# A batched row gather: four direct batches instead of five, index groups of 2, 2 and then 3, a ring of ten buffers, the seventh batch half-loaded, and first products between the index groups

## The chip, the cores and the metric

One core of one Trainium2 chip. The metric is the device time of one execution in microseconds (us); the profiler's span of the same execution is about 1.8 us shorter. Each result is compared with runs of the kernel before on the same chip and in the same rounds. "Fast" and "slow" are states of a run; for one core a run is called slow when it is over 1.5% above the fastest run of its kernel.

## The reference

```python
# x: (32, 512, 1024) float32, indices: (32, 128) int32
for b in range(32):
    result[b] = x[b, indices[b]]
```

Of each batch, 128 rows of 4 KB are picked, with repeats. Some 114 of the 128 are distinct. The kernel gathers each distinct row once into a slot and makes the repeats with a 0/1 matrix on TensorE.

## The kernel before

The first batches (`HEAD`) are gathered "directly", with their repeats, straight from the index list. For the others ("ring batches") three index steps come first, for a group of batches at a time: find the first occurrence of each index (`step0`: search on VectorE), number them (`step1`: rank), and put row numbers into slots (`step2`: slots, and the matrix `s` that spreads the slots over the output rows). A gather then fills a ring buffer, two products of 128x512 spread it, ScalarE copies the result from PSUM, and a store writes it. Batch `HALF` is special: its first 256 rows are loaded whole, early, without indices; its products have two more parts ("early products"), and its gather is half as long.

```python
HEAD, RING, GROUP, AHEAD, FAR = 5, 8, 3, 4, 1024
HALF = HEAD
# ...
pbc  = ctx.enter_context(tc.tile_pool(name="pbc",  bufs=2, space=PS))
psm  = ctx.enter_context(tc.tile_pool(name="psm",  bufs=1, space=PS))
pout = ctx.enter_context(tc.tile_pool(name="pout", bufs=4, space=PS))
# ...
for b in range(HEAD):
    gather(blocks[b], first[...] if b == 0 else idxT[:, b:b + 1], b)
    store(b)
# ...
def fetch(b):                      # gather into the ring, by the slots' row numbers
    if HEAD <= b < B:
        gather(held[(b - HEAD) % RING][:], at[:, b:b + 1], b, bounds_check=S - 1, oob_is_err=False)
# ...
def half_rows(h, last):            # the half batch: early part, or the last part and the copy
    w = slice(h * 512, (h + 1) * 512)
    if not last:
        spread[HALF, h] = pout.tile([N, 512], F32, name="ps")
    ps = spread[HALF, h]
    if last:
        pe(mm, ps[:], lhsT=spread[HALF], rhs=held[(HALF - HEAD) % RING][:, w], start=False, stop=True)
    else:
        for k in range(2):
            pe(mm, ps[:], lhsT=spread[HALF, "early"][k], rhs=early[k][:, w], start=k == 0, stop=False)
    if last:
        nc.scalar.copy(out=blocks[HALF][:, w], in_=ps[:])
# ...
step0(0)
step0(1)
for g in range(AHEAD):             # four groups, 12 batches, ahead of the first ring product
    step1(g)
    if 0 < g < AHEAD - 1:
        step0(g + 1)
    step2(g)
    for b in of_group(g):
        if b < HEAD + RING:
            fetch(b)
    if g == 0:
        half_spread()
    elif g < 3:
        half_rows(g - 1, False)    # early products between the index steps
for b in range(HEAD, B):
    spread_rows(b)
    fetch(b + RING)
    g, step = divmod(b - HEAD, GROUP)
    if g + AHEAD < GROUPS:
        (step0, step1, step2)[step](g + AHEAD)
```

The kernel holds each engine to the order of instructions written here.

## Time and profile before

| | kernel before |
|---|---|
| time | 87.41 us median of 3 (87.31 to 88.5) |
| span of the profiled run | 85.6 us |
| bytes moved by DMA | 32.91 MB |
| DMA rate from 13 us on | 416 to 419 GB/s |
| TensorE busy, 20 to 32 us | 11.98 of 12.00 us |

In the table by stretch, the last figure of a line is the DMA rate in GB/s, the one before it the busy share of the 16 DMA engines. A line of a timeline has the start and the length in us, the engine, the operation, and in brackets how long the engine was idle before it and what ended that. What the rest of the page says is read in the prediction below. Three more lines of the GpSimd timeline before give the gathers, the twelfth to the fourteenth:

```profile
18.97 1.00 POOL L121 DMA_INDIRECT u<-in_x_dram,at  x1 [1.50 <-issue]
20.27 1.00 POOL L121 DMA_INDIRECT u<-in_x_dram,at  x1 [0.30 <-issue]
22.34 1.00 POOL L121 DMA_INDIRECT u<-in_x_dram,at  x1 [1.07 <-PE bc L24]
```

### The profile page before, as it was taken

How to read it: one execution, taken by the hardware profiler on the slowest of the kernel's cores; microseconds unless marked ns; L12 is line 12 of the kernel's file. 1: busy time of each engine (PE TensorE's matmuls, PEld its weight loads, DVE VectorE, ACT ScalarE, POOL GpSimd, SP SyncE). 2: the span in 40 equal slices, each digit the busy share in tenths (PEclk: the TensorE clock that was granted, in tenths of full speed). 3: DMA queues.
4: the chain of work that ended last, by engine and by line, in shares of the span. 5: the costliest groups of instructions: out<-in, count | busy, mean ns of one | idle time of the engine just before them, and what ended most of it. 6: DMA issues, size and time to landing. Idle time of an engine off the chain costs nothing.

```text
span 85.6 us, 827 instructions
## 1 busy us (share of the span) xinstructions
PE 61.3 (72%) x189; PEld 25.3 (29%) x189; DVE 31.6 (37%) x160; ACT 40.5 (47%) x63; POOL 33.3 (39%) x43
## 2 busy tenths in 40 slices
PE   0320379576999999999878987878789888889300
PEld 0300242323434444444333433322223333323000
DVE  4498793786563864844641453000000000000000
ACT  0899930000665665555554354455544554446400
POOL 6587578727444455554332444443320000000000
PEclk9999999999999999999999999999999999999996
DMA  0799999999999999999999999999999999999980
GB/s 1 274 375 344 302 342 415 415 417 417 419 419 419 417 421 419 415 419 417 419 419 419 417 419 413 421 413 423 417 417 419 419 419 419 423 415 417 423 337 15
DMA packets 9636, 32.91 MB, mean 384 GB/s; under 512 B 1584, under 2 KB 1616, under 8 KB 9632
## 3 DMA queue, kind: packets, MB, share of 16 engines
q1 hardware_dynamic: 4736, 16.81, 48.2%
q0 software_dynamic: 4608, 15.01, 44.7%
q10 hardware_dynamic: 288, 1.05, 3.3%
q8 instruction: 1, 0.02, 0.1%
q14 instruction: 3, 0.02, 0.1%
HBM read 17.86 MB, written 16.78 MB: 404 GB/s over the span
## 4 chain that ended last, share of the span: by engine, by line
DMA 40%; PE 21%; issue 14%; DVE 14%; POOL 3%; ACT 1%; SPq 0%; POOLq 0%; DVEq 0%
DMA u<-in_x_dram,at 37%; PE ps L24 20%; DVE junk L24 3%; POOL u L121 3%; DVE pack L24 3%; DMA vals<-in_indices_dram 2%; DVE past L24 2%; DVE nth L24 2%; DVE s L24 1%; PE pos L24 1%; DVE slot L24 1%; ACT block L250 1%; DVE lead L24 1%; DVE same L24 1%; SPq L68 0%
## 5 line engine op out<-in xcount | busy, mean ns | idle before, releaser
L24 PE MATMUL ps<-u,s 128*128 128x512 f32 x108 | 52.4, 611 | 6.8 <-DMA u<-in_x_dram,at 6.2
L121 POOL DMA_INDIRECT u<-in_x_dram,at x27 | 26.9, 997 | 26.7 <-PE ps L24 5.8
L250 ACT COPY block<-ps 128x512 f32<-128x512 f32 x36 | 21.1, 585 | 18.7 <-PE ps L24 17.6
L24 PEld LDWEIGHTS ps<-u,s 128*128 128x128 f32 x108 | 18.3, 189 | 29.1 <-ACT block L250 14.8
L250 ACT COPY pair<-ps 128x512 f32<-128x512 f32 x16 | 9.4, 585 | 8.7 <-PE ps L24 7.1
L24 DVE SCALAR_TENSOR_TENSOR junk<-bc,idxF,below 128x128 f16<-128x128 f32 x27 | 8.0, 347 | 7.1 <-PE bc L24 7.1
L24 ACT COPY u<-zero 128x1024 f32<-128x1024 f32 x8 | 7.7, 1040 | 0.0
L24 PE MATMUL pos<-near,pack 128*128 128x1 f16 x27 | 2.0, 167 | 5.6 <-DVE pack L24 5.6
L240 ACT COPY block<-ps 128x512 f32<-128x512 f32 x2 | 1.2, 585 | 10.1 <-PE ps L24 10.1
L24 PE MATMUL ps<-early,same 128*128 128x512 f32 x8 | 5.7, 854 | 0.0
L24 DVE TENSOR_TENSOR pack<-turn,slot 128x384 f16<-128x384 f16 (+2 forms) x10 | 5.1, 518 | 0.3
L24 DVE TENSOR_TENSOR s<-bc,at 128x384 f32<-128x384 f32 x9 | 5.0, 558 | 0.3
L24 PEld LDWEIGHTS <-pack 128*128 128x128 f16 x27 | 1.7, 99 | 9.5 <-DVE pack L24 7.4
L24 DVE TENSOR_TENSOR past<-past,lead 128x1 f16<-128x1 f16 x25 | 4.1, 163 | 0.9
L24 PE MATMUL bc<-vf,ident 128*128 128x128 f16 x27 | 3.4, 256 | 1.3 <-DVE same L24 1.3
L121 POOL DMA_INDIRECT block<-in_x_dram,idxT x4 | 3.8, 947 | 1.3 <-issue 0.9
L24 PEld LDWEIGHTS <-ident 128*128 128x128 f16 x27 | 2.4, 111 | 4.2 <-issue 4.2
L24 DVE TENSOR_SCALAR at<-pos 128x3 int32<-128x3 f32 x9 | 1.4, 160 | 5.1 <-PE pos L24 4.8
L24 DVE CAST nth<-rk 128x3 int32<-128x3 f32 x9 | 1.4, 160 | 3.7 <-PE rk L24 3.3
L21 PE MATMUL pos<-ident,vf 128*128 128x32 f16 x1 | 0.2, 210 | 3.6 <-DVE vf L24 3.6
L24 ACT ACT_TABLE_LOAD x1 | 1.3, 1283 | 2.5 <-DVE vf L24 2.5
L24 PEld LDWEIGHTS ps<-early,same 128*128 128x128 f32 x8 | 1.9, 257 | 1.5 <-issue 1.5
(32 smaller groups left out, 18.4 us busy)
## 6 DMA issues: line engine op xcount, KB each, us to landing
out_dram<-block SPq DMA_DIRECT2D x24, 512.0 KB, 8.0
out_dram<-pair SPq DMA_DIRECT2D x4, 1024.0 KB, 11.1
early<-in_x_dram ACTq DMA_DIRECT2D x2, 512.0 KB, 3.8
u<-in_x_dram,at POOLq DMA_INDIRECT x27, 15.2
block<-in_x_dram,idxT POOLq DMA_INDIRECT x4, 6.4
vals<-in_indices_dram SPq DMA_DIRECT2D x1, 32.0 KB, 2.0
first<-in_indices_dram SPq DMA_DIRECT2D x1, 1.0 KB, 1.8
block<-in_x_dram,first POOLq DMA_INDIRECT x1, 5.2
```

What stands on the lines that cost most here:

```text
L21: self.last = do(*args, **kw)
L24: self.last = do(*args, **kw)
L121: nc.gpsimd.indirect_dma_start(out=dst, out_offset=None, in_=xf[:], in_offset=bass.IndirectOffsetOnAxis(ap=at, axis=0), element_offset=b * ...
L240: nc.scalar.copy(out=blocks[HALF][:, w], in_=ps[:])
L250: nc.scalar.copy(out=blocks[b][:, w], in_=ps[:])
```

## The change

The intent: the first ring gather should not wait for an index group of three, so the first groups have two batches and their `past` counting is off their path; one batch less is gathered with repeats; more gathers can be issued ahead of the products (ring of ten); and the first products are placed where their data lands, between the index groups. With that the half batch becomes the third ring batch, and its early products are no longer done apart. The core of the diff (index arithmetic of the ranks, the order tables and the split of `step2` into `fill_slots` and `match` are cut):

```diff
-    HEAD, RING, GROUP, AHEAD, FAR = 5, 8, 3, 4, 1024
-    HALF = HEAD
+    HEAD, RING, GROUP, FAR = 4, 10, 3, 1024
+    HALF = HEAD + 2
...
+    groups = [range(HEAD, HEAD + 2), range(HEAD + 2, HEAD + 4),
+              *(range(b, b + GROUP) for b in range(HEAD + 4, B, GROUP))]
...
-    def half_rows(h, last):
-        ...
+    def spread_rows(b, halves=range(2)):
+        for h in halves:
             w = slice(h * 512, (h + 1) * 512)
             ps = pout.tile([N, 512], F32, name="ps")
+            parts = [(spread[b], held[(b - HEAD) % RING])]
+            if b == HALF:
+                parts = [*zip(spread[b, "early"], early), *parts]
+            for i, (s, u) in enumerate(parts):
+                pe(mm, ps[:], lhsT=s, rhs=u[:, w], start=i == 0, stop=i == len(parts) - 1)
             nc.scalar.copy(out=blocks[b][:, w], in_=ps[:])
...
     step0(0)
-    step0(1)
-    for g in range(AHEAD):
-        ...
+    for g in range(2):
+        step1(g)
+        spread_indices(g + 1)
+        fill_slots(g)
+        fetch_group(g)
+        find_leads(g + 1)
+        match(g)
+    step1(2)
+    fill_slots(2)
+    fetch_group(2)
+    half_spread()
+    spread_indices(3)
+    match(2)
+    find_leads(3)
+    spread_rows(HEAD)
+    step1(3)
+    spread_rows(HEAD + 1)
+    spread_indices(4)
+    fill_slots(3)
+    fetch_group(3)
+    find_leads(4)
+    match(3)
+    step1(4)
+    spread_rows(HALF, [0])
+    spread_indices(5)
+    fill_slots(4)
+    for b in groups[4][:2]:
+        fetch(b)
+    find_leads(5)
+    match(4)
+    spread_rows(HALF, [1])
+    ...
```

More of the change, by code (lines that the diff above doesn't have):

```diff
@@ L48 @@
     N = indices.shape[1]
-    HEAD, RING, GROUP, AHEAD, FAR = 5, 8, 3, 4, 1024
-    HALF = HEAD
+    HEAD, RING, GROUP, FAR = 4, 10, 3, 1024
+    HALF = HEAD + 2
     PAIRED = range(12, 20)
-    GROUPS = (B - HEAD) // GROUP
-    assert 2 * N <= S <= FAR and (B - HEAD) % GROUP == 0
+    APART = B - 2
+    groups = [range(HEAD, HEAD + 2), range(HEAD + 2, HEAD + 4),
+              *(range(b, b + GROUP) for b in range(HEAD + 4, B, GROUP))]
+    assert HALF in groups[1] and 2 * N <= S <= FAR and groups[-1][-1] == B - 1
     const = ctx.enter_context(tc.tile_pool(name="const", bufs=1))
@@ L76 @@
     nc.gpsimd.iota(rank[:, 0], pattern=[[8, 2], [64, 2], [1, 8], [16, 4]], base=0, channel_multiplier=0)
-    for p0, p1, at0 in ((0, 36, 0), (36, 48, 112), (48, 104, 36), (104, 108, 124), (108, N, 92)):
+    for p0, p1, at0 in ((0, 38, 0), (52, 71, 44), (77, 104, 63), (105, N, 90), (71, 77, 121), (104, 105, 127)):
         nc.gpsimd.iota(rank[:, 1, p0:p1], pattern=[[1, p1 - p0]], base=at0, channel_multiplier=0)
+    twos = rank[:, 1, 38:54].rearrange("p (k a l) -> p k a l", a=2, l=2)
+    nc.gpsimd.iota(twos[:, :3, 1], pattern=[[2, 3], [1, 2]], base=38, channel_multiplier=0)
+    nc.gpsimd.iota(twos[:, :, 0], pattern=[[2, 4], [1, 2]], base=113, channel_multiplier=0)
     less = const.tile([N, 1], F32, name="less")
@@ L151, with wide, dealt_on, spread_indices @@
     nth, at = table("nth", I32), table("at", I32)
-    past = const.tile([N, B + 1], F16, name="past")
-    for b in (HEAD, B - 1):
-        dve(v.memset, past[:, b:b + 1], 0.0)
+    past = const.tile([N, len(groups)], F16, name="past")
     bcs, packs, spread = {}, {}, {}
-    def of_group(g):
-        return range(HEAD + g * GROUP, HEAD + (g + 1) * GROUP)
     def cols(t, g):
-        return t[:, HEAD + g * GROUP:HEAD + (g + 1) * GROUP]
-    def wide(t):
-        return t.rearrange("p (g o) -> p g o", o=1).to_broadcast([N, GROUP, N])
-    def step0(g):
+        return t[:, groups[g][0]:groups[g][-1] + 1]
+    def wide(t, n):
+        return t.rearrange("p (g o) -> p g o", o=1).to_broadcast([N, n, N])
+    def dealt_on(g):
+        return sum(b < APART for b in groups[g])
+    def spread_indices(g):
         bcs[g] = bc = pbc.tile([N, 4, N], F32, name="bc")
-        for k, b in enumerate(of_group(g)):
+        for k, b in enumerate(groups[g]):
             pe(mm, bc[:, k], lhsT=ident[:, b:b + 1].to_broadcast([N, N]), rhs=vf[:], start=True, stop=True)
-        for k, b in enumerate(of_group(g)):
+        if g == 0:
+            pe(mm, bc[:, GROUP], lhsT=ident[:, 0:1].to_broadcast([N, N]), rhs=turn[:, 0], start=True, stop=True)
+    def find_leads(g):
+        bc = bcs[g]
+        for k, b in enumerate(groups[g]):
             junk = junkp.tile([N, N], F16, name="junk")
@@ L174, in step0 @@
                 op0=ALU.is_equal, op1=ALU.mult, accum_out=cnt[:, b:b + 1])
-        if HALF in of_group(g):
+        if HALF in groups[g]:
             c = slice(HALF, HALF + 1)
@@ L179, in step0 @@
         dve(v.tensor_scalar, out=cols(lead, g), in0=cols(cnt, g), scalar1=0.0, scalar2=None, op0=ALU.is_equal)
-        for b in of_group(g):
-            if b < B - 2:
-                dve(v.tensor_tensor, out=past[:, b + 1:b + 2], in0=past[:, b:b + 1], in1=lead[:, b:b + 1], op=ALU.add)
+    def step0(g):
+        spread_indices(g)
+        find_leads(g)
     def step1(g):
         rk = psm.tile([N, GROUP], F32, name="rk")
-        pe(mm, rk[:], lhsT=above[:], rhs=cols(lead, g), start=True, stop=False)
-        pe(mm, rk[:], lhsT=every[:], rhs=cols(past, g), start=False, stop=True)
-        dve(v.tensor_copy, out=cols(nth, g), in_=rk[:])
+        n, like = len(groups[g]), dealt_on(g)
+        earlier = [(k, lead[:, groups[g][0]:groups[g][0] + like - k]) for k in range(1, like)]
+        if g:
+            earlier.append((0, past[:, g:g + 1].to_broadcast([N, like])))
+        pe(mm, rk[:, :n], lhsT=above[:], rhs=cols(lead, g), start=True, stop=not earlier)
+        for i, (k, more) in enumerate(earlier):
+            pe(mm, rk[:, k:like], lhsT=every[:], rhs=more, start=False, stop=i == len(earlier) - 1)
+        dve(v.tensor_copy, out=cols(nth, g), in_=rk[:, :n])
         dve(v.tensor_scalar, out=cols(nth, g), in0=cols(nth, g), scalar1=N - 1, scalar2=None, op0=ALU.bitwise_and)
@@ L193, in step1 @@
         packs[g] = pack = junkp.tile([N, GROUP, N], F16, name="pack")
-        like = GROUP - (g == GROUPS - 1)
-        dve(v.tensor_tensor, out=pack[:, :like], in0=turn[:, 0:1].to_broadcast([N, like, N]),
-            in1=wide(cols(slot, g))[:, :like], op=ALU.is_equal)
-        if like < GROUP:
-            dve(v.tensor_tensor, out=pack[:, like:], in0=turn[:, 1:2], in1=wide(cols(slot, g))[:, like:], op=ALU.is_equal)
-    def step2(g):
-        pos = psm.tile([N, GROUP], F32, name="pos")
-        for k, b in enumerate(of_group(g)):
-            pe(mm, pos[:, k:k + 1], lhsT=packs[g][:, k], rhs=near[:, b:b + 1], start=True, stop=True)
-        dve(v.tensor_scalar, out=cols(at, g), in0=pos[:], scalar1=float(FAR), scalar2=None, op0=ALU.add)
-        s = pick.tile([N, GROUP, N], F32, name=f"s{g}")
-        dve(v.tensor_tensor, out=s[:], in0=bcs[g][:, :GROUP], in1=wide(cols(at, g)), op=ALU.is_equal)
-        for k, b in enumerate(of_group(g)):
-            spread[b] = s[:, k]
+        table = turn[:, 0:1] if g else bcs[0][:, GROUP:]
@@ new lines, in step1, with count_on @@
+        dve(v.tensor_tensor, out=pack[:, :like], in0=table.to_broadcast([N, like, N]),
+            in1=wide(cols(slot, g)[:, :like], like), op=ALU.is_equal)
+        if like < n:
+            dve(v.tensor_tensor, out=pack[:, like:], in0=turn[:, 1:2].to_broadcast([N, n - like, N]),
+                in1=wide(cols(slot, g)[:, like:], n - like), op=ALU.is_equal)
+    def count_on(g):
+        c = past[:, g + 1:g + 2]
+        for k in range(len(groups[g])):
+            more = cols(lead, g)[:, k:k + 1]
+            if g == k == 0:
+                dve(v.tensor_copy, out=c, in_=more)
+            else:
+                dve(v.tensor_tensor, out=c, in0=c if k else past[:, g:g + 1], in1=more, op=ALU.add)
@@ new lines, in fill_slots, with match @@
+    def fill_slots(g):
+        pos = psm.tile([N, GROUP], F32, name="pos")
+        for k, b in enumerate(groups[g]):
+            pe(mm, pos[:, k:k + 1], lhsT=packs[g][:, k], rhs=near[:, b:b + 1], start=True, stop=True)
+        dve(v.tensor_scalar, out=cols(at, g), in0=pos[:, :len(groups[g])], scalar1=float(FAR), scalar2=None, op0=ALU.add)
+    def match(g):
+        n = len(groups[g])
+        s = pick.tile([N, n, N], F32, name=f"s{g}")
+        dve(v.tensor_tensor, out=s[:], in0=bcs[g][:, :n], in1=wide(cols(at, g), n), op=ALU.is_equal)
+        if g < len(groups) - 1:
+            count_on(g)
+        for k, b in enumerate(groups[g]):
+            spread[b] = s[:, k]
@@ L224, in half_spread @@
         for k in range(2):
-            dve(v.tensor_scalar, out=same[:, k], in0=bcs[0][:, HALF - HEAD], scalar1=less[:], scalar2=float(k * N),
+            dve(v.tensor_scalar, out=same[:, k], in0=bcs[1][:, HALF - groups[1][0]], scalar1=less[:], scalar2=float(k * N),
                 op0=ALU.add, op1=ALU.is_equal)
         spread[HALF, "early"] = [same[:, k] for k in range(2)]
-    def half_rows(h, last):
-        w = slice(h * 512, (h + 1) * 512)
-        if not last:
-            spread[HALF, h] = pout.tile([N, 512], F32, name="ps")
-        ps = spread[HALF, h]
-        if last:
-            pe(mm, ps[:], lhsT=spread[HALF], rhs=held[(HALF - HEAD) % RING][:, w], start=False, stop=True)
-        else:
-            for k in range(2):
-                pe(mm, ps[:], lhsT=spread[HALF, "early"][k], rhs=early[k][:, w], start=k == 0, stop=False)
-        if last:
-            nc.scalar.copy(out=blocks[HALF][:, w], in_=ps[:])
@@ L242, in spread_rows @@
-    def spread_rows(b):
-        for h in range(2):
-            if b == HALF:
-                half_rows(h, True)
-                continue
+    def spread_rows(b, halves=range(2)):
+        for h in halves:
             w = slice(h * 512, (h + 1) * 512)
             ps = pout.tile([N, 512], F32, name="ps")
-            pe(mm, ps[:], lhsT=spread[b], rhs=held[(b - HEAD) % RING][:, w], start=True, stop=True)
-            nc.scalar.copy(out=blocks[b][:, w], in_=ps[:])
-        store(b)
+            parts = [(spread[b], held[(b - HEAD) % RING])]
[3 more added lines that the diff above has]
+                pe(mm, ps[:], lhsT=s, rhs=u[:, w], start=i == 0, stop=i == len(parts) - 1)
+            nc.scalar.copy(out=blocks[b][:, w], in_=ps[:])
+        if 1 in halves:
+            store(b)
@@ L253, with fetch_group @@
+    def fetch_group(g):
+        for b in groups[g]:
+            fetch(b)
     step0(0)
-    step0(1)
-    for g in range(AHEAD):
+    for g in range(2):
         step1(g)
-        if 0 < g < AHEAD - 1:
-            step0(g + 1)
-        step2(g)
-        for b in of_group(g):
-            if b < HEAD + RING:
-                fetch(b)
-        if g == 0:
-            half_spread()
-        elif g < 3:
-            half_rows(g - 1, False)
-    for b in range(HEAD, B):
+        spread_indices(g + 1)
+        fill_slots(g)
+        fetch_group(g)
+        find_leads(g + 1)
+        match(g)
@@ new lines @@
+    step1(2)
[18 more added lines that the diff above has]
+    for b in groups[4][:2]:
+        fetch(b)
+    find_leads(5)
+    match(4)
+    spread_rows(HALF, [1])
+    fetch(groups[4][2])
@@ L268 @@
+    step1(5)
+    spread_rows(HEAD + 3)
+    spread_indices(6)
+    fill_slots(5)
+    match(5)
+    fetch(HEAD + 3 + RING)
+    for b in range(HEAD + 4, B):
+        g, step = divmod(b - HEAD - 4, GROUP)
         spread_rows(b)
+        if g + 6 < len(groups):
+            (find_leads if g == step == 0 else (step0, step1, step2)[step])(g + 6)
         fetch(b + RING)
-        g, step = divmod(b - HEAD, GROUP)
-        if g + AHEAD < GROUPS:
-            (step0, step1, step2)[step](g + AHEAD)
 _INS = ['x', 'indices']
```

## The prediction

> **What bounds the kernel now.** I read the page first (time slices), then the table of busy time by stretch, then the timelines of GpSimd and TensorE. The page's slices of 2.14 us:
>
> ```profile
> PE   0320379576999999999878987878789888889300
> DMA  0799999999999999999999999999999999999980
> GB/s 1 274 375 344 302 342 415 415 417 417 419 419 419 417 421 419 415 419 417 419 419 419 417 419 413 421 413 423 417 417 419 419 419 419 423 415 417 423 337 15
> DMA packets 9636, 32.91 MB, mean 384 GB/s; under 512 B 1584, under 2 KB 1616, under 8 KB 9632
> ```
>
> The reader is to see that the DMA engines are busy from the second slice to the last but one, and that from the seventh slice (12.8 us) to the end the rate is flat at 415 to 423 GB/s. Nothing that an engine computes shows in it: the kernel is bound by the bytes moved. The only stretch below the plateau, start and tail apart, lies before 12 us. The table by stretch (stretch, length, busy time of PE, PEld, DVE, ACT, POOL, clock, DMA share, GB/s) gives its size:
>
> ```profile
> 8.00:9.00 1.00, 0.27 (x5) 0.24 (x6) 0.64 (x2) 1.00 (x2) 0.94 (x1) 1.00 1.01 328
> 9.00:10.00 1.00, 0.03 (x2) 0.00 (x0) 0.95 (x4) 1.00 (x2) 0.04 (x2) 1.00 1.05 344
> 10.00:11.00 1.00, 0.48 (x3) 0.21 (x2) 0.90 (x6) 1.00 (x2) 0.97 (x1) 1.00 0.94 238
> 11.00:12.00 1.00, 0.60 (x4) 0.58 (x5) 1.00 (x6) 0.47 (x1) 0.73 (x1) 1.00 0.91 311
> 12.00:13.00 1.00, 1.00 (x2) 0.34 (x1) 0.86 (x7) 0.00 (x0) 0.70 (x2) 1.00 1.00 406
> 30.00:50.00 20.00, 18.04 (x61) 8.00 (x60) 10.14 (x49) 10.86 (x19) 9.48 (x10) 1.00 1.03 418
> ```
>
> Against 418 the four stretches from 8 to 12 lack 90 + 74 + 180 + 107 = 451 KB, or 1.08 us; those from 4 to 8 (397, 365, 373, 336) lack 201 KB, or 0.48 us. So 1.5 us is all that a better beginning can give. The GpSimd timeline shows the gathers' starts and the gap that the first index group causes:
>
> ```profile
> 8.06 0.95 POOL L121 DMA_INDIRECT block<-in_x_dram,idxT  x1 [0.30 <-issue]
> 9.96 1.01 POOL L121 DMA_INDIRECT u<-in_x_dram,at  x1 [0.96 <-ACT u L24]
> 11.27 1.00 POOL L121 DMA_INDIRECT u<-in_x_dram,at  x1 [0.30 <-issue]
> ```
>
> Back to back they start 1.30 us apart (a 1.00 us issue and 0.30 us). The sixth starts 1.90 us after the fifth. The page's ACT release is not the cause (that zeroing was long done); the DVE timeline has the row numbers `at` done at 9.17, and the gather starts 0.79 us later.
>
> **What the Trainium skill says.** "DMA: Bandwidth & Descriptors", section "Where 436 GB/s comes from", gives 435 GB/s as the ceiling of the fabric; it also says that the HBM side, about 358, binds HBM transfers. This trace agrees with the first (418, 96%) and not with the second. The same page, "Queues, rings and completion order", says that each engine goes round the queues that have work, packet by packet. The trace agrees: from 14 to 16 us stores moved 0.43 MB and gathers 0.39 MB. "TensorE: Matmul & The Clock Gate", section "The HAM clock gate", says that the array runs at half rate until some 3.4 us of sustained work. Two stretches of the TensorE timeline agree: the same four matmuls, first cold, then warm.
>
> ```profile
> 11.50 3.76 PE L24 MATMUL ps<-early,same 128*128 128x512 f32 x4
> 16.67 1.96 PE L24 MATMUL ps<-early,same 128*128 128x512 f32 x4
> ```
>
> Cold, one takes 0.853 us from start to start, warm 0.428.
>
> **The change part by part.** *Bytes.* One batch less is gathered with its duplicates. Counting the distinct indices, the rows read fall from 3920 to 3905: 61 KB, 0.15 us at 418. Gain 0.15 us.
>
> *First groups.* The first group has two batches, its `past` steps are gone from its path, and the second group's search no longer stands before it on DVE. From the search's start at 4.2: two searches at 0.27, lead 0.2, two small matmuls 0.4, three small DVE steps 0.6, pack of 256 columns 0.43 (the 384 took 0.56), pos 0.25, at 0.2. That ends near 6.9 instead of 9.17. The fifth gather (now batch 4, no longer direct) can follow the fourth at 8.06, and the sixth at 9.36 instead of 9.96. The sixth also carries a whole batch, where before the half batch (50 rows, 205 KB) stood there. The second group's numbers: two searches, count and lead 1.05, match 0.43, two counts 0.35, then the same chain of about 1.7, near 10.5; seventh gather near 11.25, eighth 12.55, as before (11.27, 12.58). Of the 451 KB I give back a quarter, 0.25 us: in most of that stretch the engines were busy (share 0.91 to 1.05) with a backlog queued, so much of the low rate is not missing work, and the gathers up to the fifth are issued as before.
>
> *Third group.* Three searches 1.05, match 0.43, two counts 0.35, chain 1.9: near 14.2, plus 0.79, so the ninth gather starts near 15.0; it was 13.88. Tenth and eleventh 16.3 and 17.6 (15.18, 16.47).
>
> *Fourth group and first products.* Here TensorE's order decides. The rank of the fourth group stands after the products of batch 4, and its slots after those of batch 5. Batch 4's gather stands where the fifth stood; that one landed at 17.0. The products that warmed TensorE at 11.5 are gone, they are now done together with the half batch, so those of batch 4 run cold: 4 x 0.853 = 3.4 us, to 20.5. Batch 5's take 1.7 to 2.5, to about 22.6; slots and numbers by 23.1; twelfth gather near 23.9, where it was 18.97. The next follow at 1.3 us: 25.2, 26.5, 27.8 (before: 20.27, 22.34, 24.28).
>
> *Backlog.* By 18.6 us the changed kernel has issued 5.78 MB of reads and 2.10 MB of stores (four direct). The trace before had moved 3.16 MB by 12 us and moves 0.418 a microsecond after, so 7.0 MB by 21.3. Left: 0.8 MB. Store of batch 4 (0.52) comes at about 21.3, of batch 5 at 23.3; gathers of 0.46 to 0.49 from 24.9 on, every 1.3 us (some 360 GB/s); the half batch, 12 matmuls x 0.428 = 5.1 us, brings its store only near 29. Between 23 and 30 the backlog is 0.2 to 0.9 MB. A gather needs 5 us or more from start to landing even early on (the page's direct gathers: 6.4 us), so a backlog of 0.3 MB (five packets per engine) will leave some engines idle. The kernel before had 2.4 to 2.8 MB there. I charge 0.3 us (12% of the rate over 2.5 us); with TensorE warm at once it would be 0, with batch 5 cold as well up to 1.5.
>
> *Later.* Twenty more small matmuls (the order counts 126 matmul rows against 104, of which two are products) and 1.9 us of zeroing for two buffers lie beside the transfers. TensorE ran 43 of the 50 us from 30 to 80, so a lag of 3 or 4 us at batch 8 can be made up: 1.8 us of products per batch against 2.37 us of transfers. Ten buffers give no more than eight gathers at a time, since the order of instructions shows each gather waiting for the landing of the eighth before it. Cost 0.
>
> Sum: 87.4 - 0.15 - 0.25 + 0.3 = 87.3 us.
>
> **The rivals.** *The beginning was the whole loss*: the new order fills 8 to 12 us, and the feed at 23 to 30 holds. For it: the gap of 1.90 us lies just ahead of the 238 GB/s, and the change was built around it. Against: the share of 0.94 and 1.05 in it. Time: 87.4 - 1.1 - 0.15 = 86.2. *A starved DMA takes its place*: TensorE, waiting for batch 4 and cold, holds back the fourth group. For it: the cold 3.4 us and the order. Against: 0.8 MB of backlog at 21 us, and the products may start before 17. Time: 87.4 - 0.4 + 1.5 = 88.5. *Nothing shows*: the transfers hide both; 87.2, the bytes alone. *TensorE becomes the bound at the end*: batch 8 near 32, then 23 batches of 1.83 to 1.95 us, ends near 76, where the kernel before ends its products at 79.9; unlikely.
>
> **Range and chances.** The first two rivals set the edges, 86.2 and 88.5; I take 86.3 to 88.5 as the range of 8 in 10. Faster by 2% means under 85.7, which is more than the whole loss of the beginning: 0.05. Slower by 2% means over 89.2, with the feed broken for 2 us: 0.09. Within: 0.86.
>
> **What would show it.** Right: gathers five to eight near 8.06, 9.4, 11.3 and 12.6; first product near 17 and cold; twelfth gather near 23.9; GB/s above 330 from 10 to 12 and a dip below 400 somewhere from 22 to 30; 418 after it. Wrong: no dip there (then faster, near 86.5), or a first product that is warm or much earlier; or a plateau other than 418, or a TensorE that is busy to the end while the DMA share falls.

## The result, and the profile after

| | before | changed |
|---|---|---|
| time, median (lowest to highest) | 87.44 us (87.31 to 88.5, 4 runs) | 92.52 us (91.82 to 93.07, 4 runs) |
| ratio of the fast runs | | 1.0549, 95% interval 1.0427 to 1.067 |
| span of the profiled run | 85.6 us | 89.9 us |
| bytes moved by DMA | 32.91 MB | 32.85 MB |

The ratio is the mean time of one kernel's fast runs over that of the other's of the same rounds, so it is not quite the ratio of the medians. The changed kernel is 5.5% slower, outside the range of 86.3 to 88.5 us. The profiled run, 91.82 us, is the fastest of the four, with a mean granted clock of TensorE of 0.971 (1 is full speed); the other three, 92.05 to 93.07 us, had 0.944 to 0.946, and no trace of them is kept.

The page's slices of the changed kernel, 2.25 us each:

```profile
PE   0212213089919999999999999999999988850000
...
DMA  0799989999999988899999999999999999999970
GB/s 2 254 401 283 242 295 427 410 412 418 418 419 283 359 266 281 310 410 421 416 412 418 416 423 418 418 421 416 419 423 414 419 425 414 421 419 418 427 325 31
```

The plateau is the same as before. It is reached at 13 us, left at 27 us, and found again at 38 us: five slices at 266 to 359 GB/s. This is the dip that the prediction had looked for between 22 and 30 us, but deeper and longer. TensorE's row shows two nearly idle slices: the 0 just before its first products (16 to 18 us), and the 1 before the half batch's products (25 to 27 us), with a solid row of nines after it. The table by stretch of the changed kernel:

```profile
8.00:13.00 5.00, 1.34 (x12) 0.71 (x12) 3.88 (x22) 5.00 (x6) 3.72 (x5) 1.00 0.91 270
13.00:20.00 7.00, 2.40 (x8) 1.23 (x9) 3.09 (x16) 0.36 (x1) 3.60 (x4) 1.00 1.03 417
20.00:26.00 6.00, 4.82 (x17) 1.99 (x15) 2.17 (x13) 2.34 (x4) 0.22 (x1) 1.00 1.03 417
26.00:32.00 6.00, 5.22 (x21) 2.60 (x22) 3.69 (x20) 0.59 (x1) 3.87 (x5) 1.00 0.97 340
32.00:40.00 8.00, 8.00 (x32) 3.56 (x31) 4.51 (x22) 4.53 (x8) 4.91 (x5) 1.00 0.89 310
40.00:50.00 10.00, 10.00 (x42) 4.52 (x41) 5.42 (x28) 6.04 (x12) 5.00 (x5) 1.00 1.02 415
```

Against 418 GB/s the two stretches from 26 to 40 us lack 78 x 6 + 108 x 8 = 1332 KB, which is 3.2 us. GpSimd's timeline says when the gathers came:

```profile
17.47 1.00 POOL L127 DMA_INDIRECT u<-in_x_dram,at  x1 [0.30 <-issue]
25.78 1.00 POOL L127 DMA_INDIRECT u<-in_x_dram,at  x1 [7.32 <-ACT block L275]
27.09 1.00 POOL L127 DMA_INDIRECT u<-in_x_dram,at  x1 [0.30 <-issue]
28.39 1.00 POOL L127 DMA_INDIRECT u<-in_x_dram,at  x1 [0.30 <-issue]
30.61 1.00 POOL L127 DMA_INDIRECT u<-in_x_dram,at  x1 [1.22 <-DVE at L24]
```

The twelfth gather starts at 25.78 instead of 18.97, the fifteenth at 30.61 instead of 24.28. (The release by ACT is the page's guess among several semaphores; the row numbers `at` of that group were written at 24.85 to 25.01.) TensorE's chain in the same time, batch 4, batch 5, then the two halves of the half batch:

```profile
18.32 3.78 PE L24 MATMUL ps<-u,s 128*128 128x512 f32 x4 [3.17 <-DMA u<-in_x_dram,at]
...
22.05 2.55 PE L24 MATMUL ps<-u,s 128*128 128x512 f32 x4
...
27.10 1.96 PE L24 MATMUL ps<-early,same 128*128 128x512 f32 x4
28.90 1.02 PE L24 MATMUL ps<-u,s 128*128 128x512 f32 x2
...
30.00 1.96 PE L24 MATMUL ps<-early,same 128*128 128x512 f32 x4
31.80 1.02 PE L24 MATMUL ps<-u,s 128*128 128x512 f32 x2
```

From the landing of batch 4 to the end of the half batch's products, 14.5 us go by for three batches. The kernel before did its first three ring batches from 20.11 to 25.9, in 5.8 us:

```profile
20.11 1.96 PE L24 MATMUL ps<-u,s 128*128 128x512 f32 x4
...
23.93 1.96 PE L24 MATMUL ps<-u,s 128*128 128x512 f32 x4
```

Its early products had been done from 11.5 to 18.6, where TensorE had little else to do. Of the 14.5 us the early products are 8 x 0.428 = 3.4 us of warm work; the rest, beside the products that both kernels have, is the cold clock (3.78 for the first batch) and waits for the index steps.

**Two kinds of start.** The same changed kernel, run again unedited (e11), had this page:

```profile
GB/s 0 202 395 388 382 338 414 412 416 418 420 408 310 382 284 317 399 379 416 410 410 416 420 422 420 418 423 414 420 418 422 418 420 420 418 418 420 422 321 11
```

The slices three to six, 395 388 382 338, were 401 283 242 295 in the first profile. From 8 to 13 us the rate is 361 GB/s in one and 270 in the other, for the same program. Both kinds turn up with both kernels: unedited or little edited, the kernel before had 325 in its profile, 271 and 274 in two of its variants. I call them quick and slow starts. So the first profiles, before (quick, 87.44 us) and changed (slow, 91.82), differ by a start as well. Like with like, the changed kernel with a quick start took 89.79 us, 2.35 more, and lacked (418 - 335) x 6 + (418 - 357) x 8 = 986 KB, or 2.36 us, from 26 to 40: in this pair the dip accounts for the whole difference. The two runs are of different rounds, and the kernel before went from 86.87 to 88.72 us in the rounds of e11, so the close match is in part luck. Twelve profiled runs, with the shortfall worked out from the table by stretch in the same way (26 to 40 us, against 418):

| run | time us | GB/s 8-13 | GB/s 26-32 | GB/s 32-40 | shortfall us | time less shortfall |
|---|---|---|---|---|---|---|
| before | 87.44 | 325 | 419 | 418 | 0 | 87.4 |
| e11, changed again | 89.79 | 361 | 335 | 357 | 2.4 | 87.4 |
| e1, slots first | 91.09 | 352 | 327 | 323 | 3.1 | 88.0 |
| e10, short warm-up | 90.46 | 342 | 315 | 324 | 3.3 | 87.2 |
| e12, no early half products | 87.69 | 350 | 395 | 413 | 0.4 | 87.3 |
| e14, half products in idle time | 88.61 | 370 | 337 | 404 | 1.4 | 87.2 |
| e8, before with half products late | 87.89 | 342 | 386 | 405 | 0.7 | 87.2 |
| changed, first profile | 91.82 | 270 | 340 | 310 | 3.2 | 88.6 |
| e13, changed again | 91.06 | 273 | 355 | 346 | 2.3 | 88.8 |
| e15, mended order | 88.36 | 288 | 417 | 417 | 0 | 88.3 |
| e6, the same, earlier | 89.58 | 256 | 417 | 414 | 0.1 | 89.5 |
| e4, before with ring of ten | 87.94 | 271 | 418 | 418 | 0 | 87.9 |

Less its shortfall, every quick start in the table ends at 87.2 to 88.0 and every slow one at 87.9 to 89.5, whichever kernel. In all 18 profiles the second gather, the first that needs the whole index table, starts at 4.20 to 4.45 us in a quick start and at 4.67 to 5.10 in a slow one. Why the table comes later, and whether that is what slows the start, is not known. Both kinds turn up with the same program, so the change does not decide it; whether it alters how often each comes is not shown. The profiles of e6 and e14 fell on runs that count as slow by the 1.5% rule, so verdicts below rest on the ratios of fast runs, and this table only on what the traces show. Not in it are six more slow starts: e2, e3, e5, e7, e9 and e16, with shortfalls of 2.5, 3.7, 1.6, 2.7, 0.4 and 4.7 us; less these they end at 88.4 to 89.6.

**The backlog.** From the trace one can add up what had been issued by a time (gathers counted by their rows at the end of their issue, stores at theirs) and take off what had been moved. In MB:

| at us | before | changed, quick start (e11) | mended order (e15) |
|---|---|---|---|
| 20 | 2.9 | 1.7 | 2.2 |
| 24 | 2.7 | 1.1 | 2.0 |
| 26 | 2.8 | 0.75 | 2.1 |
| 28 | 3.0 | 1.0 | 2.3 |
| 30 | 3.1 | 0.8 | 2.5 |
| 32 | 3.3 | 1.1 | 2.6 |
| 36 | 3.6 | 1.9 | 2.9 |

In e11 the dip begins where the backlog has gone under about 1 MB, and ends some 2 us after it has come over 1.5. That end is no rule: in e14 (below) the backlog was 0.8 MB at 26, 1.8 at 30 and 2.1 at 32 us, and the rate still lay at 329 to 374 GB/s until 35.6.

**The clock goes down a second time in some runs.** The trace of e16, which repeats e1, has the granted clock at one half from 28.2 to 31.6 us, in the middle of the half batch's products; e1 has it whole there. The fifteenth gather came at 32.93 us in e16 and at 28.75 in e1, and the shortfall was 4.7 us against 3.1. Some 1.3 us of that delay is e16's slow start, so the clock may have its share in the rest. e5, e7 and e10 have such a stretch too. The dip doesn't need it: the traces of the changed kernel (the first profile, e11, e13) have the whole clock from 21 to 23 us on. But three of the four first runs of the changed kernel had a low mean clock (0.944 to 0.946), as had the three longest of six in e13 and the three longest of seven in e16, all at 0.946 to 0.948. So the 5.1 us between the medians probably hold a share of the clock beside the dip and the kind of start. e16's profile is of a slow run and no experiment set this apart, so its size stays open.

### The profile page after: what moved, and what is told of

The parts are those of the page before. It is cut to its first block, busy times and chain, and to the rows that moved or that the text cites.

```text
span 89.9 us, 892 instructions
## 1 busy us (share of the span) xinstructions
PE 61.9 (69%) x213; PEld 27.2 (30%) x213; DVE 32.6 (36%) x167; ACT 43.7 (49%) x67; POOL 33.9 (38%) x46
## 2 busy tenths in 40 slices
DMA packets 9636, 32.85 MB, mean 366 GB/s; under 512 B 1599, under 2 KB 1631, under 8 KB 9632
## 4 chain that ended last, share of the span: by engine, by line
PE 40%; DMA 32%; issue 5%; DVE 5%; POOL 4%; ACT 1%; SPq 0%; POOLq 0%; DVEq 0%
PE ps L24 37%; DMA u<-in_x_dram,at 29%; POOL u L127 4%; DMA vals<-in_indices_dram 2%; DVE junk L24 2%; PE bc L24 1%; PE rk L24 1%; DVE lead L24 1%; ACT block L275 1%; PE pos L24 1%; DVE vf L24 1%; DVE pack L24 0%; SPq L71 0%; DVE nth L24 0%; DVE at L24 0%
## 5 line engine op out<-in xcount | busy, mean ns | idle before, releaser
L24 PE MATMUL ps<-u,s 128*128 128x512 f32 x112 | 54.4, 628 | 4.1 <-DMA u<-in_x_dram,at 4.1
L127 POOL DMA_INDIRECT u<-in_x_dram,at x28 | 28.2, 1006 | 26.1 <-ACT block L275 7.3
L24 PEld LDWEIGHTS ps<-u,s 128*128 128x128 f32 x112 | 20.5, 197 | 25.9 <-issue 18.4
L24 ACT COPY u<-zero 128x1024 f32<-128x1024 f32 x10 | 9.5, 1038 | 0.0
L24 DVE CAST nth<-rk 128x3 int32<-128x3 f32 (+1 forms) x10 | 1.6, 162 | 10.9 <-PE rk L24 10.7
L24 DVE TENSOR_TENSOR s<-bc,at 128x384 f32<-128x384 f32 (+1 forms) x10 | 5.3, 527 | 0.2
L24 PE MATMUL rk<-lead,above 128*128 128x3 f16 (+1 forms) x10 | 1.8, 176 | 4.8 <-DVE lead L24 3.5
L24 DVE TENSOR_SCALAR at<-pos 128x3 int32<-128x3 f32 (+1 forms) x10 | 1.6, 161 | 7.8 <-PE pos L24 7.8
L24 PE MATMUL ps<-early,same 128*128 128x512 f32 x8 | 3.9, 612 | 0.0
L24 PEld LDWEIGHTS <-every 128*128 128x128 f16 x25 | 1.5, 102 | 3.6 <-issue 3.6
```

The source lines that it names most:

```text
L24: self.last = do(*args, **kw)
L127: nc.gpsimd.indirect_dma_start(out=dst, out_offset=None, in_=xf[:], in_offset=bass.IndirectOffsetOnAxis(ap=at, axis=0), element_offset=b * ...
```

## The experiments

Theory A: TensorE's order holds back the slots of the fourth group. Rival B: the half batch's products starve the DMA. Rival C: the slower first 13 us. Theory D, that the half batch's early products do the harm where they stand now, came after the first twelve runs. Ratios are to the kernel before in the same rounds, fast runs.

**e1, slots first.** The changed kernel with the fourth group's rank, slots and gathers ahead of the products.

```diff
     find_leads(3)
-    spread_rows(HEAD)
     step1(3)
-    spread_rows(HEAD + 1)
-    spread_indices(4)
     fill_slots(3)
     fetch_group(3)
+    spread_rows(HEAD)
+    spread_rows(HEAD + 1)
+    spread_indices(4)
     find_leads(4)
```

> Changed kernel with the rank, slots and gathers of the fourth group moved ahead of the products of the first two ring batches. Theory A (TensorE's order holds the fourth group back, so the DMA is underfed from 26 to 40 us): the twelfth gather starts near 19.2 us instead of 25.78, the rate from 26 to 40 us rises from 323 to about 390 GB/s, and the time falls from 92.5 to 89 to 90 us (the half batch still holds back the fifth group). Rival B (the half batch's three products, 5.4 us of TensorE in a row, starve the DMA whatever comes before): the dip stays from 28 to 36 us and the time stays over 91.5 us. Rival C (the slower first 13 us are the loss): the time falls by under 0.5 us.

Measured: 91.13 us median (90.97 to 92.92), ratio 1.0388 (1.0289 to 1.0486). GpSimd's timeline:

```profile
18.42 1.00 POOL L127 DMA_INDIRECT u<-in_x_dram,at  x1 [0.88 <-issue]
19.72 1.00 POOL L127 DMA_INDIRECT u<-in_x_dram,at  x1 [0.30 <-issue]
21.03 1.00 POOL L127 DMA_INDIRECT u<-in_x_dram,at  x1 [0.30 <-issue]
28.75 1.00 POOL L127 DMA_INDIRECT u<-in_x_dram,at  x1 [6.72 <-DVE at L24]
```

The twelfth to fourteenth gathers came over 5 us earlier, as meant, and the fifteenth did not move: 28.75, against 28.70 in the changed kernel with the same kind of start. Three gathers earlier fill the queue earlier; they add no bytes to it by 30 us. The dip stayed (3.1 us). Theory A as stated fails: its 89 to 90 us were not reached.

**e2 and e3, with throwaway matmuls.** Eight matmuls whose result nobody reads, in front of the first products, to warm the clock; e3 has them together with e1.

```diff
     find_leads(3)
+    for h in range(2):
+        w = slice(h * 512, (h + 1) * 512)
+        warm = pout.tile([N, 512], F32, name="ps")
+        for k in range(2):
+            pe(mm, warm[:], lhsT=spread[HALF, "early"][k], rhs=early[k][:, w], start=k == 0, stop=k == 1)
     spread_rows(HEAD)
```

> Changed kernel with eight throwaway matmuls (the first product's operands, a result that nobody reads) ahead of the first products, in TensorE's idle time from 15 to 18 us: takes away the cold clock alone, adds no DMA work. Theory A with the cold clock as a cause: the products of the first ring batch take 1.8 instead of 3.6 us, those of the second 1.8 instead of 2.4, the twelfth gather starts near 23.4 instead of 25.78 us, and the time falls to about 90.5 us. If the clock doesn't matter: within 0.5 us of 92.5.

> Both edits: fourth group's slots ahead of the products, and the throwaway matmuls. Theory A: the dip from 26 to 40 us goes but for a little, rate there over 405 GB/s, time 87.5 to 88.5 us. Rival B: dip at 28 to 34 us remains, time 90 us or more. Rival C: over 91.5 us.

Measured: e2 91.45 us (91.37 to 93.62), ratio 1.0428 (1.033 to 1.0525); e3 93.96 us (92.59 to 94.43), 1.0735 (1.0649 to 1.082). Both were badly made. The eight began cold and took from 15.34 to 20.84 us in e2, where TensorE was idle only until the first landing near 18.5. In e2 the twelfth gather came at 25.64, as in the changed kernel; in e3 the throwaway work stood ahead of the fourth group's rank, and the fifteenth gather came at 31.77. So e2 does not isolate the clock, though its first products did come out warm (1.88 us) and its dip was 2.5 us all the same; e3 shows only that this work ahead of the fourth group's rank made e1 slower still (1.0735, against 1.0388 for e1 in the same rounds).

**e5, the delay in the kernel before.** The third group's rank and slots behind the first and second ring products, everything else as it was.

```diff
     for g in range(AHEAD):
+        if g == 2:
+            spread_rows(HEAD)
         step1(g)
         if 0 < g < AHEAD - 1:
             step0(g + 1)
+        if g == 2:
+            spread_rows(HEAD + 1)
         step2(g)
...
-        elif g < 3:
-            half_rows(g - 1, False)
+        elif g == 1:
+            half_rows(0, False)
+            half_rows(1, False)
     for b in range(HEAD, B):
-        spread_rows(b)
+        if b > HEAD + 1:
+            spread_rows(b)
```

> The kernel before with the delay alone: the third group's rank stands after the products of the first ring batch and its slots after those of the second (five direct batches, ring of eight, groups of three and early half products as before). Theory A: the twelfth gather starts near 24 instead of 18.97 us, a dip below 380 GB/s appears somewhere from 24 to 36 us, and the time rises by 1 to 3 us to 88.5 to 90.5. Rivals B and C: it stays at 87.4 within 0.5 us.

Measured: 90.29 us (89.29 to 91.06), ratio 1.024 (1.0106 to 1.0375). Twelfth gather at 25.87; 412 GB/s from 26 to 32 and 339 from 32 to 40. So late gathers do it in the kernel before too, with its five direct batches and ring of eight; rival C isn't needed for the loss. (The clock was at one half from 29.5 to 32.9 us in this profile; its share is not set apart.)

**e6 and e15, the mended order.** The changed kernel with another order on TensorE: the half batch's early products in four pieces in idle time, and the fourth group's slots and the fifth's search ahead of the ring products. The early products need a PSUM buffer for each half that stays open, so `pout` has two buffers instead of four. The lines that the edit removes are left out here.

```diff
+    pout = ctx.enter_context(tc.tile_pool(name="pout", bufs=2, space=PS))
+    phalf = ctx.enter_context(tc.tile_pool(name="phalf", bufs=2, space=PS))
...
     find_leads(3)
+    half_early(0, 0)
     step1(3)
+    half_early(0, 1)
     fill_slots(3)
     fetch_group(3)
     spread_indices(4)
     find_leads(4)
+    half_early(1, 0)
     match(3)
     step1(4)
+    half_early(1, 1)
+    spread_rows(HEAD)
+    spread_indices(5)
+    fill_slots(4)
+    fetch(groups[4][0])
...
```

> Changed kernel (four direct batches, groups of 2, 2, 3, ring of ten, same half batch) with another order on TensorE alone: rank and slots of the fourth group and the search of the fifth ahead of all ring products; the half batch's early products in four pieces between those steps, in two PSUM banks of their own (two are left for the other products). Theory A (slots queued behind products and half products keep the gathers late): twelfth gather near 19 us, fifteenth near 24 to 25 (it was 30.61), no stretch below 400 GB/s after 14 us, time back to the kernel before within 1%, 87 to 88 us. If the rest of the change (ring, groups, direct batches) costs by itself: 89.5 us or more with the dip gone.

> e6 again (half products in idle time and slots of the fourth group and search of the fifth ahead). Both theories: no dip, 87.5 to 89 us; the distance from e14 is what the order of the slots is worth, 0.5 to 1 us by theory D.

Measured: e6 88.69 us (87.58 to 89.58), ratio 1.0064 (0.9941 to 1.0187); e15 88.84 us (87.83 to 89.86), 1.0043 (0.9957 to 1.0129). The table by stretch of e15, a slow start:

```profile
8.00:13.00 5.00, 1.33 (x12) 0.71 (x12) 3.88 (x22) 5.00 (x6) 3.72 (x5) 1.00 0.92 288
...
20.00:26.00 6.00, 5.17 (x23) 2.46 (x24) 3.73 (x20) 1.89 (x4) 3.59 (x4) 1.00 1.03 419
26.00:32.00 6.00, 5.81 (x20) 2.43 (x20) 3.31 (x17) 3.38 (x6) 2.99 (x3) 1.00 1.03 417
32.00:40.00 8.00, 8.00 (x32) 3.47 (x32) 3.54 (x18) 5.10 (x9) 4.17 (x5) 1.00 1.03 417
```

No dip is left, though everything else of the change is in it: direct batches, groups, ring, half batch. So the order on TensorE is the cause, and the rest of the change costs at most about 1.3% and gains at most 0.4% (the interval of e15).

**e7 and e12, without the early half products.** The changed kernel, batch 6 wrong, all transfers and waits kept.

```diff
             parts = [(spread[b], held[(b - HEAD) % RING])]
-            if b == HALF:
-                parts = [*zip(spread[b, "early"], early), *parts]
```

> Changed kernel with the half batch's two early products left out (batch 6 comes out wrong on purpose; all transfers and waits as they were): 8 matmuls, 3.4 us of TensorE less between the fifth and sixth groups. Theory A with the half products as a cause: the fifteenth gather starts near 28.9 instead of 30.61 us, the eighteenth near 32 instead of 35.4, time 90.5 to 91.3 us. If only the fourth group's order matters: within 0.5 us of 92.5.

> The changed kernel itself, unedited, on the same chip as the next three, so that each of them has it beside it. Every theory: 91.5 to 93 us.

> The changed kernel without the half batch's two early products (batch 6 wrong on purpose) once more, because the first time its runs fell into two heaps, 88.0 and 88.8 against 91.0 and 91.2 us. If 3.4 us less of TensorE work between the fifth and sixth groups is a cause: 1 to 3 us below the changed kernel of the same rounds. If the heaps are noise of the chip: the changed kernel shows two heaps as well.

Measured: e7 88.02 and 88.84 us in its fast runs, 91.02 and 91.19 in its slow ones, ratio 1.0076 (0.9938 to 1.0214). On another chip and in five rounds: the changed kernel itself (e11) 91.16 us (89.79 to 93.03), 1.0345 (1.0239 to 1.045); without the early products (e12) 88.81 us (87.69 to 90.58), 1.0155 (1.0087 to 1.0224). Taking away 3.4 us of TensorE's work gains 2.4 us by the medians, 1.9% by the fast runs. The gathers of e12, fifteenth to seventeenth:

```profile
26.53 1.00 POOL L127 DMA_INDIRECT u<-in_x_dram,at  x1 [0.30 <-DVE junk L24]
27.84 1.00 POOL L127 DMA_INDIRECT u<-in_x_dram,at  x1 [0.31 <-issue]
29.14 1.00 POOL L127 DMA_INDIRECT u<-in_x_dram,at  x1 [0.30 <-PE ps L24]
```

In e11, which had a quick start too, these stood at 28.70, 30.00 and 31.31. The half batch's store came at 27.1 instead of 31.6 us.

**e9, slots first and no early half products.** Both edits together.

> Both: the fourth group's rank, slots and gathers ahead of the products, and no early half products (batch 6 wrong on purpose). Theory A: the two causes add up; twelfth gather near 19, fifteenth near 27 instead of 28.75 (slots first alone) and 30.61 us (changed kernel), rate from 26 to 40 us about 370 GB/s, time 88.5 to 90 us, under either edit alone. If the half products don't matter once the slots come first: within 0.5 us of slots first alone (91.1).

Measured: 90.19 us (89.25 to 91.83), ratio 1.0316 (1.0255 to 1.0378): the prediction that the two add up is a miss, it is slower than e12. Its profile (a slow start) has little of a dip, 404 and 406 GB/s, and its fifteenth gather stands at 28.21. Why its runs are slower than those of e12 stays open; its only profile cannot tell whether its unprofiled runs dipped.

**e10, a shorter warm-up.** Four throwaway matmuls.

> The changed kernel with four throwaway matmuls (a result that nobody reads) from about 15.2 to 18.6 us, short enough to fit TensorE's idle time, unlike the eight of the earlier try, which ran to 20.8 and ate what they gained. If the cold clock is part of the cause: first products take about 2 instead of 3.6 us, twelfth gather near 24 instead of 25.78, time 0.5 to 1.5 us below the changed kernel of the same rounds. If not: the same within 0.4 us.

Measured: 90.42 us (90.04 to 91.89), ratio 1.0321 (1.0268 to 1.0374), beside 1.0345 for e11. The first products did get warm (2.01 us instead of 3.78), the twelfth gather came at 23.20 instead of 23.88 and the fifteenth at 29.66 instead of 28.70. TensorE waited from 22 to 24.5 for index steps and went cold again (clock at one half from 25.2 to 28.6), and the half batch's first half was slow:

```profile
24.45 3.05 PE L24 MATMUL ps<-early,same 128*128 128x512 f32 x4
27.29 1.67 PE L24 MATMUL ps<-u,s 128*128 128x512 f32 x2
```

In e11 these took 1.95 and 1.02. So the cold clock of the first products is not shown to cost anything in the time, while in the half batch's place it delayed the fifteenth gather, and the dip was 3.3 us instead of 2.4.

**e8 and e4, one part of the change in the kernel before.** e8 does the early half products at the half batch's turn, e4 has a ring of ten (and issues a gather after the index step of its turn, which ten buffers need).

```diff
e8:
-        elif g < 3:
-            half_rows(g - 1, False)
...
             if b == HALF:
+                half_rows(h, False)
                 half_rows(h, True)
e4:
-    HEAD, RING, GROUP, AHEAD, FAR = 5, 8, 3, 4, 1024
+    HEAD, RING, GROUP, AHEAD, FAR = 5, 10, 3, 4, 1024
```

> Kernel before with one part of the change alone: the half batch's early products done together with its last one, at its turn (no early warm-up of TensorE; slots of four groups still ahead of all products). Theory A: slots stay ahead, so the twelfth and thirteenth gathers stay near 19 and 20.3 us; the first products run cold and 3.4 us longer, gathers from the fourteenth on come 3 to 5 us later (27 instead of 22.34); a small dip; time up by 0.3 to 1.5 us, 87.7 to 89. If the half products are the main cause: up by 3 us or more.

> Kernel before with a ring of ten buffers instead of eight, nothing else but that each gather is issued after the index step of its turn. Theory A: no change, 87.4 us within 0.5, since the DMA rate is at its plateau of 418 GB/s after 13 us and each gather still waits for the landing of the eighth before it. If the ring costs by itself (longer zeroing beside the first transfers, reads that run ahead of stores): 88.5 us or more.

Measured: e8 87.93 us (87.57 to 88.39), ratio 1.0024 (0.9925 to 1.0124); e4 88.59 us (87.94 to 88.95), 1.0108 (1.0017 to 1.0199). In e8 the fourteenth gather moved from 22.34 to 26.14, the backlog fell to 0.8 MB at 26 us, and the rate was 386 and 405 GB/s from 26 to 40: a shallow dip of 0.7 us that the times do not resolve. There the half batch is the first ring batch, so no store waits behind two others and it, and a fifth direct store is queued at 17.0. Late half products alone are thus not enough. That it takes them in third place, with the slots of later groups between them, is an argument; no run tests it alone. The ring alone shows no dip; it may cost about 1% (interval 0.2 to 2.0%).

**e13, e14, e16, the two edits of the mended order apart.** e14 moves only the half products:

```diff
+    half_spread()
     step1(2)
+    half_early(0, 0)
     fill_slots(2)
     fetch_group(2)
-    half_spread()
     spread_indices(3)
     match(2)
     find_leads(3)
+    half_early(0, 1)
+    half_early(1, 0)
     spread_rows(HEAD)
     step1(3)
+    half_early(1, 1)
     spread_rows(HEAD + 1)
```

(with the two PSUM pools of e6). e13 is the changed kernel, e16 is e1 again, e15 is above; all four on one chip, five rounds.

> The changed kernel, unedited, as the measure for the next three. Every theory: 90 to 93 us, dip of 2.4 us (quick start) to 3.2 us (slow start) from 26 to 40 us.

> The changed kernel with the half batch's early products alone moved: three of their four pieces into TensorE's idle time from 12 to 18 us, the fourth ahead of the second ring products, in two PSUM banks of their own; slots of the fourth group stay behind the products; result right. Theory D (TensorE's work between the first landing and about 35 us is too much, and the half products are the part that the change moved into it): the half batch's turn shrinks from 5.1 to 1.7 us, its store comes near 29 instead of 31.6 to 33.5, the eighteenth gather near 31 instead of 33.5, the dip falls by half or more, time 1 to 2 us below the changed kernel. Theory A (slots behind products): no gain over 0.5 us.

> e1 again (slots and gathers of the fourth group first, nothing else). Theory D: within 0.7 us of the changed kernel of the same rounds, since the fifteenth gather and the half batch's store stay where they were. Theory A: 1.5 us or more below it.

| run | median us (range) | ratio, 95% interval |
|---|---|---|
| e13, changed | 92.30 (91.06 to 94.48) | 1.0466, 1.039 to 1.0542 |
| e14, half products in idle time | 88.56 (87.14 to 89.6) | 0.9961, 0.985 to 1.0072 |
| e15, mended order | 88.84 (87.83 to 89.86) | 1.0043, 0.9957 to 1.0129 |
| e16, slots first | 91.67 (90.43 to 94.31) | 1.0337, 1.0248 to 1.0426 |

Moving the half products alone brings the time back, 3.7 us by the medians. The ratio of e14 rests on two fast runs only, but its six runs (up to 89.6 us) all lie below all six of e13 (from 91.06). Theory A, which had the slots as the cause and no gain here, fails again: the slots' order alone gains 0.6 us by the medians and its interval overlaps that of e13, and on top of e14 it gains nothing in the time (e15). TensorE's timeline of e14, its early pieces and the half batch's turn:

```profile
12.22 2.07 PE L24 MATMUL hs<-early,same 128*128 128x512 f32 x2
...
14.48 3.63 PE L24 MATMUL hs<-early,same 128*128 128x512 f32 x4
...
19.77 1.10 PE L24 MATMUL hs<-early,same 128*128 128x512 f32 x2
...
25.02 1.10 PE L24 MATMUL hs<-u,s 128*128 128x512 f32 x2
...
26.50 1.10 PE L24 MATMUL hs<-u,s 128*128 128x512 f32 x2
```

The three first pieces lie where the changed kernel's TensorE was idle, and the half batch's products are done at 27.6 us, instead of 30.9 in e11 (a quick start as well). They warm the clock on the way: batch 4's products took 1.88 us in e14. The profile of e14 fell on a run that counts as slow (88.61 us, against a fastest of 87.14), and still has a dip of 1.4 us, so e14 does not always clear it; e15's profile does. Against e11 the dip shrank by 1.0 us, less than the 3.7 us between the medians; the traces do not account for the rest.

No version here beats the kernel before: the best, e14, has a ratio of 0.9961 with 1 inside its interval.

## Why the prediction was wrong

- **The bound** (bytes at a plateau of 418 GB/s, only the beginning below it): right. Before and after share the plateau to within 2 GB/s.
- **Bytes and first groups, gain 0.15 and 0.25 us**: the issues came nearly as worked out (gathers five to eight at 8.44, 9.75, 11.31, 12.61 with a slow start; 8.08, 9.39, 10.69, 11.99 with a quick one; foretold 8.06, 9.36, 11.25, 12.55). A gain cannot be seen; the kind of start moves the time by more. The sign "above 330 from 10 to 12" failed: 229 and 152 GB/s in the first profile, 369 and 266 in e11. One figure was misread: the half batch's gather before has 60 rows (246 KB), not 50; the count of 3920 rows has it right.
- **Fourth group and first products**: right in kind and nearly in size. Cold first products: 3.78 against 3.4 us; twelfth gather 23.88 with a quick start; 25.78 with a slow one, 1.9 us later than the foretold 23.9.
- **The next gathers, "at 1.3 us: 25.2, 26.5, 27.8"**: the last is wrong. The fifteenth gather belongs to the fifth group, whose slots stand behind the first half of the half batch: 28.70 to 30.61. The half batch's store, foretold near 29, came at 31.6 to 33.5.
- **The step that failed is the charge for the backlog: "I charge 0.3 us (12% of the rate over 2.5 us)".** The backlog itself was foretold as 0.2 to 0.9 MB and was 0.5 to 1.1 from 26 to 32 us (0.5 in the first profile, at 28). Its price was 2.4 us with a quick start and 3.2 with a slow one: the rate fell by 15 to 26%, and for 14 us, not by an eighth for 2.5. The rider "with TensorE warm at once it would be 0" was wrong too: in e2 and e10 the first products took 1.9 and 2.0 us, and the dips were 2.5 and 3.3 us.
- **"Later ... can be made up. Cost 0"**: half right. TensorE's lag was made up (its last product ended at 79.9 in both), but the DMA had lost its bytes by then, and a kernel at its byte rate never gets them back. I took a lag for harmless because the lagging engine had slack; the lag sat in the feed of the engine without slack.
- **The rivals**: "a starved DMA takes its place" was the right one, and was given 88.5 us and 1.5 us of cost, where the dip took 2.4 to 3.2 and the medians differ by 5.1. What I had not seen is that the half products, which cost the changed kernel most (e14), had been nearly free before: their old place was idle time. I had named them as warm-up and as 5.1 us, and had charged neither.

What stays open: why e9 was slower than e12; how much of the 5.1 us between the medians is the second fall of the clock; whether the warm clock in e14 has a share of its own; and what makes a start slow.

## What to carry to other kernels

When one engine or the DMA is the bound, judge a reordering by the backlog in front of it: add up what is issued and what is moved at a few times, and where the backlog is small (here under about 1 MB) expect the rate to stay down for long, not for a moment: here it was lower by 15 to 26% for 14 us. Work on an engine that is not the bound was free here where that engine was idle, and cost 3.7 us by the medians in another place: before merging instructions that were apart, look whether the gap that they filled was free and whether the place they go to feeds the bound. Before comparing two profiles, check with a repeat that they are of the same kind of run.

## What the Trainium skill lacked or had wrong

- "DMA: Bandwidth & Descriptors", section "Where 436 GB/s comes from": it has about 358 GB/s as what binds transfers between HBM and SBUF. Taken alone that does not hold here: 415 to 419 GB/s held for over 60 us, reads and writes mixed, one core at work. The measured rates in the section just above it on the same page, up to 425 GB/s for a single core, do fit.
- The same page says to issue a DMA early and to overlap, but not how much must be queued to keep the rate: here the runs whose backlog stayed at 2.0 MB and more (before, e15) held 415 to 419 GB/s, and 0.75 to 1.4 MB gave 335 (e11) and 386 (e8) from 26 to 32 us.
- "TensorE: Matmul & The Clock Gate", section "The HAM clock gate", was borne out (0.853 against 0.428 us a matmul). It has about 3.4 us without work as what takes the clock down again. In e10 a wait of 2.4 us between products, with small matmuls in it, was followed by half the clock for 3.4 us and 3.05 us for four matmuls instead of 1.96; in the first profile of the changed kernel a wait of 2.5 us was not.
- No page: two kinds of start of the same program, 270 or 361 GB/s from 8 to 13 us, over 1 us of the time in the changed kernel. None says how to tell them (here by the rate from 8 to 13 us, or by the second gather's start, up to 4.45 us or from 4.67 on).
